# A hybrid decoder layer: both key halves of a stick-breaking head in one accumulator, one stick tile per row, softmax sums added once per head

## The chip, the cores and the metric

The kernel runs on one core of one Trainium2 chip. The metric is the device time of one execution in microseconds (us), and lower is better. The core has four engines that compute: TensorE (PE in the profile, with its weight loads as PEld), VectorE (DVE), ScalarE (ACT) and GpSimd (POOL). SyncE (SP) issues the transfers.

## The reference, cut to what matters

One layer with 2048 tokens and width 1024. A normalised input is projected for two groups of eight heads that work side by side: causal softmax attention over low-rank latents (MLA, group 0), and stick-breaking attention (group 1). Both outputs are normalised, joined, projected back to the residual, and a gated feed-forward layer follows. The stick-breaking group is

```python
z = jnp.einsum("bhqd,bhkd->bhqk", qb.astype(jnp.float32), kf) * scale
log_beta = jax.nn.log_sigmoid(z)
log_one_minus = jnp.where(strict, jax.nn.log_sigmoid(-z), 0.0)
suffix = lax.cumsum(log_one_minus, axis=3, reverse=True) - log_one_minus
a = jnp.where(strict, jnp.exp(log_beta + suffix), 0.0)
return jnp.einsum("bhqk,bhkd->bhqd", a, vf)
```

so that the weight of a key is its own sigmoid times the product of the sigmoids of the negated scores of all later keys: a running product from the last key to the first. Its output is a plain sum over keys, where softmax needs the row's maximum and sum.

## The kernel before, in words

**Stages.** The 2048 tokens are four blocks (b = 0 to 3) of 512, each of four rows (r) of 128. `ORDER` (L87) lists the stages: projections P0 to P3, attention A0 to A3, feed-forward F0, F1, and F for blocks 2 and 3 as a pair by a seven-product scheme. Every operand is split into a high and a low part, and three products replace one.

**Order of the work.** Nothing is issued while these stages are written down. Each call on `plan` is recorded as a task (`record`, L205) with the earlier tasks that it needs, a rank that comes from its stage, and a planned cost (`price`, L243). `order` (L288) then plays a list schedule over five engines: of the tasks that are ready in the plan, an engine takes the one with the lowest key. A transfer counts as landed `DMA_DONE` (L68, used at L412) after its planned time on the wire. `issue` (L458) emits the instructions in that order, and each engine works through its own list strictly in that order. So planned costs set which dense product stands between which attention steps, and an engine whose next instruction is not ready waits, whatever else is ready. The plan also hands out buffers: eight PSUM banks, of which one (`O_B`, L51) is for the attention output `ot`, two for scores, two for transposes, and the others for dense products (`acc`).

**Attention.** `attention` (L781) goes through heads and both groups. Keys come in halves of `SW` = 1024, the later half (c0 = 1024) first; only blocks 2 and 3 have two halves. Each half is a `Unit` (L696): it loads keys and values, and `step` (L774) runs its four rows. A row has one or two pieces of up to 512 keys (`pieces`, L602).

`mla_row` (L632), for each piece: scores into PSUM, `reduce_max` on VectorE; then with two pieces the maximum of both, a scaling `nm`, an exponential on ScalarE per piece with its row sum, and an add of the two sums into `sm`.

`sb_row` (L658), last piece first: scores, two sigmoids on ScalarE, then the running product (`tensor_tensor_scan`) on VectorE into a tile `tb` of 513 columns, whose last column holds what the later piece left: 1, a copy of the later piece's first column, or a copy of the `carry` of the later half. GpSimd then multiplies it into `p`. Two `tb` tiles exist (`NT_BUFS`, L60).

`mix` (L607) takes two rows at a time: it transposes `p` on TensorE into `pt`, splits it (`ph` on ScalarE, `pl` on VectorE), and adds `v` times it into `ot`. After the fourth row `finish` (L727) copies `ot` to `os` (ScalarE), transposes it with four transposes (TensorE, `po`), adds its two parts (ScalarE copy, VectorE add), and keeps the result (`o1`) if it was the first half, or joins both halves and stores it. For stick-breaking the join is one more VectorE add.

`fop_places` (L1016) lists the places for feed-forward operands of the last stage, which lie in attention's buffers once it is over; among them were two `nb` and two `tb` tiles.

Of the kernel before, what the change touches and what calls it, by code (L numbers as in the profile page):

```python
# [66 lines left out]
DMA_RATE = 300.0  # L67
DMA_DONE = 910.0  # L68
NORM_LATE = 1
# [113 lines left out]
class Plan:  # L183
# [21 lines left out]
    def record(self, engine, method, args, kwargs):  # L205
# [8 lines left out]
        for k, v in views:  # L214
            write = k in (first, "accum_out")
            base, region = v.base, v.region or v.base.whole
            if base not in t.bases:
                t.bases.append(base)
            for old, oreg, owrite in base.seen:
                if k == first and engine == "tensor" == old.engine and kwargs.get("start"):  # L220
                    t.needs.add(old.index)
                if (write or owrite) and old is not t and all(a < d and c < b for (a, b), (c, d) in zip(region, oreg)):
                    t.needs.add(old.index)
            if write:
                base.seen = [s for s in base.seen if s[0] is t or not all(a <= c and d <= b for (a, b), (c, d) in
                                                                           zip(region, s[1]))]
            base.seen.append((t, region, write))
        for b in t.bases:
            b.uses += 1
# [13 lines left out]
    def price(self, t):  # L243
# [3 lines left out]
        if t.engine == "tensor":  # L247
# [3 lines left out]
            if t.method == "transpose":  # L251
                cost = 109 if exact else 60
            else:
                cost = 160 if exact else max(58, 10 + 0.4246 * n)
        elif t.engine == "scalar":
# [220 lines left out]
def layer(ctx, tc, x, positions, inv_freq, norm_mix, w_in, q_latent_norm, w_uq,  # L476
# [73 lines left out]
    with ExitStack() as s:  # L550
# [55 lines left out]

        def mix(ot, r0, rows, v, c0):  # L607

            at = [{k0 // P + i: p[:, i * P:(i + 1) * P] for p, k0, n in row for i in range(n // P)} for row in rows]
            js = sorted(at[1])  # L610
            for ja in js[::2]:
# [11 lines left out]
                for half in (ph, pl):  # L623
                    x = 0
                    for j, rs in pair:
                        w = len(rs) * P
                        o0 = (r0 + rs[0]) * P
                        plan.tensor.matmul(ot[:, o0:o0 + w], lhsT=v[:, j - c0 // P, :], rhs=half[:, x:x + w],
                                           start=j == js[0] and half is ph, stop=j == js[-1] and half is pl)
                        x += w  # L630

        def mla_row(r, b, c0, k, q, mx, sm):  # L632
            rs_ = slice(r * P, (r + 1) * P)
            lhs = [(q[0][:, rs_], k, c0), (q[1][:, rs_], k, c0), (q[2][:, rs_], kr, 0)]
            m2 = wk.tile([P, 2], F32, tag="m2", name="m2", bufs=3)
            nm = wk.tile([P, 1], F32, tag="nm", name="nm", bufs=3)
            s2 = wk.tile([P, 2], F32, tag="s2", name="s2", bufs=3)
            parts = pieces(b, r, c0)
# [10 lines left out]
            for i, (k0, n, last) in enumerate(parts):  # L649
                p = pp.tile([P, 512], F32, tag="p", name="p")  # L650
                to = s2[:, i:i + 1] if len(parts) == 2 else sm[:, r:r + 1]
                plan.scalar.activation(p[:, :n], pss[i][:, :n], AF.Exp, bias=nm, scale=SC_M, accum_out=to)
                res.append((p, k0, n))
            if len(parts) == 2:
                plan.vector.tensor_tensor(out=sm[:, r:r + 1], in0=s2[:, 0:1], in1=s2[:, 1:2], op=ALU.add)
            return res

        def sb_row(r, b, c0, k, q, carry, carry_out):  # L658
            rs_ = slice(r * P, (r + 1) * P)
            lhs = [(q[0][:, rs_], k, c0), (q[1][:, rs_], k, c0)]  # L660
            after = None if carry is None else carry[:, r:r + 1]
            res = []
            for k0, n, last in reversed(pieces(b, r, c0)):
                p = pp.tile([P, 512], F32, tag="p", name="p")
                ps = sp.tile([P, 512], F32, tag="s", name="ps_s")
                scores(ps, k0, n, False, lhs)
                tb = wk.tile([P, 513], F32, tag="tb", name="tb", bufs=NT_BUFS)
                plan.scalar.activation(p[:, :n], ps[:, :n], AF.Sigmoid, scale=SC_S)
                plan.scalar.activation(ps[:, :n], ps[:, :n], AF.Sigmoid, scale=-SC_S)
                if after is None:  # L670
                    plan.vector.memset(tb[:, n:n + 1], 1.0)
                else:
                    plan.vector.tensor_copy(tb[:, n:n + 1], after)
                rev, other = ps[:, :n][:, ::-1], p[:, :n][:, ::-1]
                if last:
                    d = n - P
                    plan.gpsimd.tensor_tensor(out=p[:, d:n], in0=p[:, d:n], in1=below, op=ALU.mult)
                    plan.vector.tensor_tensor_scan(tb[:, d:n][:, ::-1], rev[:, :P], beyond[:, ::-1], tb[:, n:n + 1],
                                                 op0=ALU.mult, op1=ALU.max)
                    if d:  # L680
                        plan.vector.tensor_tensor_scan(tb[:, :d][:, ::-1], rev[:, P:], other[:, P:], tb[:, d:d + 1],
                                                     op0=ALU.mult, op1=ALU.bypass)
                else:
                    plan.vector.tensor_tensor_scan(tb[:, :n][:, ::-1], rev, other, tb[:, n:n + 1],
                                                 op0=ALU.mult, op1=ALU.bypass)
                plan.gpsimd.tensor_tensor(out=p[:, :n], in0=p[:, :n], in1=tb[:, 1:n + 1], op=ALU.mult)
                after = tb[:, 0:1]
                res.append((p, k0, n))
            if carry_out is not None:
                plan.vector.tensor_copy(carry_out[:, r:r + 1], after)  # L690
            return res
# [4 lines left out]
        class Unit:  # L696
# [11 lines left out]
            def rows(self, c0, k, v):  # L708
                self.c0, self.v, self.p = c0, v, []
                if self.g == 0:  # L710
                    self.mx = st.tile([P, BT], F32, tag="mx", name="mx")
                    self.sm = st.tile([P, BT], F32, tag="sm", name="sm")
                    return [lambda r=r: mla_row(r, self.b, c0, k, self.q, self.mx, self.sm) for r in range(BT)]
# [4 lines left out]
            def add(self, r, res):  # L718
                self.p.append(res)
                if r % 2:  # L720
                    if r == 1:
                        self.ot = op.tile([P, TB], F32, tag="ot", name="ot")
                    mix(self.ot, r - 1, self.p[-2:], self.v, self.c0)
                if r == BT - 1:
                    self.finish()

            def finish(self):  # L727
# [9 lines left out]
                plan.scalar.activation(po, pt[:, :, :VD], AF.Copy)  # L737
                plan.vector.tensor_tensor(out=po, in0=pt[:, :, VD:], in1=po, op=ALU.add)
                if self.c0:
                    self.o1 = po  # L740
                    return
                o = None if self.g else wk.tile([P, BT, VD], F32, tag="o", name="o")
                if self.g:
                    o = po
                    if self.prev:
                        plan.vector.tensor_tensor(out=o, in0=po, in1=self.prev.o1, op=ALU.add)
                else:
# [4 lines left out]
                    else:  # L752
                        o1, m1, s1 = self.prev.o1, self.prev.mx, self.prev.sm
                        top = st.tile([P, BT], F32, tag="top", name="top")
                        f = st.tile([P, 2, BT], F32, tag="f", name="f")
                        plan.vector.tensor_tensor(out=top, in0=self.mx, in1=m1, op=ALU.max)
                        plan.vector.tensor_tensor(out=f[:, 0], in0=self.mx, in1=top, op=ALU.subtract)
                        plan.vector.tensor_tensor(out=f[:, 1], in0=m1, in1=top, op=ALU.subtract)
                        plan.scalar.activation(f, f, AF.Exp, scale=SC_M)
                        plan.vector.tensor_tensor(out=den, in0=f[:, 0], in1=self.sm, op=ALU.mult)  # L760
# [251 lines left out]
        def place(pool, tag, n):  # L1012
            bufs = {"rt": RT_BUFS, "ph": PH_BUFS, "pl": PH_BUFS, "nb": NT_BUFS, "tb": NT_BUFS}.get(tag)
# [515 lines left out]
```

## Time and profile before

| what | us |
|---|---|
| three runs | 3042.35, 3046.29 (median), 3048.05 |
| the profiled execution, its own time | 3046.05 |
| its span, first to last instruction | 3044.3 |
| TensorE busy in it | 2966.1 |
| VectorE, ScalarE, GpSimd busy | 2382.7, 1786.1, 574.8 |

Busy TensorE means that at least one matmul was in flight. All instructions have the line of the function that emits the plan, so they are told apart by the names of their tiles: `os<-ot` is the copy of the attention output, `po<-ident,os` its transposes, and so on. Attention runs from about 146 us to 1945 us of the span, with projections and feed-forward work of other blocks between its steps; behind it only feed-forward work and output projections are left.

### The profile page before, as it was taken

To read this page: it belongs to the slowest core of one execution; us is meant where nothing else is said; L and a number is where in the kernel's file an instruction comes from. 1 tells how busy PE (TensorE), PEld (TensorE's weight loads), DVE (VectorE), ACT (ScalarE), POOL (GpSimd) and SP (SyncE) were. 2 spreads that over 40 slices of the span, in tenths; PEclk is the share of its full clock that TensorE was granted. 3 is DMA by queue.
4 is the path that set the end of the run, shared out by engine and by line. 5 is a ranking of instruction groups with operands and counts; after the bars stand their busy time and mean duration, and the time that the engine had idled before them with its cause. 6 is when DMAs were issued, how large, how long until landed. Compare 5 with 4: busy or idle time off the path is not lost.

```text
span 3044.3 us, 47607 instructions
## 1 busy us (share of the span) xinstructions
PE 2966.1 (97%) x16372; PEld 2544.5 (84%) x16372; DVE 2382.7 (78%) x4927; ACT 1786.1 (59%) x3858; POOL 574.8 (19%) x619
## 2 busy tenths in 40 slices
PE   8899999999999999999999999999999999999998
PEld 7889888888888888888888888888888788888887
DVE  6567878888989889798978889655657877777777
ACT  5557777777777767777767677544534333233323
POOL 0002221222313314140504123000003100100111
PEclk9999999999999999999999999999999999999999
DMA  6987876677574434434333535355633312111212
GB/s 201 267 259 229 254 224 191 189 226 230 155 206 124 128 108 135 140 117 146 112 105 119 154 118 175 112 176 166 187 110 119 112 55 63 49 48 50 63 49 83
DMA packets 403432, 437.78 MB, mean 144 GB/s; under 512 B 76875, under 2 KB 296054, under 8 KB 403190
## 3 DMA queue, kind: packets, MB, share of 16 engines
q1 hardware_dynamic: 403190, 434.74, 47.3%
q8 instruction: 129, 2.11, 0.3%
q14 instruction: 113, 0.93, 0.1%
HBM read 350.78 MB, written 83.89 MB: 143 GB/s over the span
## 4 chain that ended last, share of the span: by engine, by line
PE 85%; DVE 5%; DMA 5%; ACT 3%; issue 1%; SPq 0%; POOL 0%; ACTq 0%; POOLq 0%; DVEq 0%
PE ps_gu L472 15%; PE ps_d L472 15%; PE ps_m L472 14%; PE ps_s L472 10%; PE ot L472 8%; PE pt L472 7%; PE ps_o L472 5%; PE ps_q L472 5%; PE ps_v L472 2%; PE ps_lat L472 2%; DVE tb L472 1%; PE po L472 1%; PE ps_t L472 1%; DVE acc L472 1%; DMA raw<-in_w_in 1%
## 5 line engine op out<-in xcount | busy, mean ns | idle before, releaser
L472 ACT ACTIVATE whi<-raw 128x512 fp32r<-128x512 f32 (+1 forms) x726 | 448.3, 626 | 581.9 <-PE ps_d L472 208.9
L472 DVE TENSOR_TENSOR wlo<-raw,whi 128x512 fp32r<-128x512 f32 (+1 forms) x726 | 527.2, 734 | 184.9 <-ACT whi L472 177.5
L472 ACT ACTIVATE ph<-pt 128x512 fp32r<-128x512 f32 (+1 forms) x576 | 315.8, 577 | 137.0 <-PE pt L472 123.0
L472 POOL TENSOR_TENSOR p<-p,tb 128x512 f32<-128x512 f32 (+3 forms) x320 | 326.6, 1021 | 351.4 <-DVE tb L472 337.0
L472 PE MATMUL ps_s<-k,q 128*128 128x512 f32 (+3 forms) x1280 | 380.8, 375 | 11.6 <-DMA k<-d_mk 7.3
L472 DVE TENSOR_TENSOR pl<-pt,ph 128x512 fp32r<-128x512 f32 (+1 forms) x576 | 369.9, 650 | 26.3 <-ACT ph L472 23.5
L472 PE MATMUL pt<-ident,p 128*128 128x128 f32 x2176 | 365.5, 275 | 6.2 <-POOL p L472 4.3
L472 PE MATMUL ps_m<-fop,whi 128*128 128x512 f32 (+1 forms) x1254 | 358.8, 375 | 0.0
L472 DVE TENSOR_TENSOR_SCAN tb<-ps_s,tb,p 128x512 f32<-128x512 f32 (+3 forms) x288 | 315.4, 1096 | 6.6 <-ACT ps_s L472 3.1
L472 DVE TENSOR_TENSOR acc<-acc,ps_d 128x512 f32<-128x512 f32 x352 | 235.2, 681 | 78.5 <-PE ps_d L472 74.8
L472 PE MATMUL ps_gu<-tl,whi 128*128 128x512 f32 x704 | 282.8, 402 | 0.0
L472 PEld LDWEIGHTS pt<-ident,p 128*128 128x128 f32 x2176 | 259.7, 141 | 26.6 <-POOL p L472 5.5
L472 PE MATMUL ps_gu<-th,whi 128*128 128x512 f32 x704 | 281.9, 401 | 0.0
L472 PE MATMUL ps_gu<-th,wlo 128*128 128x512 f32 x704 | 281.6, 400 | 0.0
L472 PE MATMUL ps_d<-whi,hh 128*128 128x512 f32 x704 | 278.5, 396 | 0.6 <-ACT hh L472 0.6
L472 PE MATMUL ps_d<-wlo,hh 128*128 128x512 f32 x704 | 277.6, 394 | 0.0
L472 PE MATMUL ps_d<-whi,hl 128*128 128x512 f32 x704 | 272.8, 394 | 0.0
L472 PEld LDWEIGHTS ps_m<-fop,whi 128*128 128x128 f32 x1254 | 227.6, 189 | 45.6
L472 PEld LDWEIGHTS ps_s<-k,q 128*128 128x128 f32 x1280 | 225.1, 190 | 45.3 <-DMA k<-d_mk 7.7
L472 PE MATMUL ot<-pl,v 128*128 128x256 f32 (+1 forms) x1152 | 245.9, 293 | 3.2 <-DVE pl L472 2.3
L472 PE MATMUL ot<-ph,v 128*128 128x256 f32 (+1 forms) x1152 | 232.9, 283 | 12.9 <-ACT ph L472 12.6
L472 PEld LDWEIGHTS ot<-pl,v 128*128 128x128 f32 x1152 | 201.7, 192 | 38.6 <-DVE pl L472 6.5
(222 smaller groups left out, 6178.0 us busy)
## 6 DMA issues: line engine op xcount, KB each, us to landing
raw<-in_w_gate SPq DMA_DIRECT2D x66, 512.0 KB, 4.6
raw<-in_w_up SPq DMA_DIRECT2D x66, 512.0 KB, 3.8
raw<-in_w_down SPq DMA_DIRECT2D x66, 512.0 KB, 3.7
raw<-in_w_o SPq DMA_DIRECT2D x64, 512.0 KB, 4.0
raw<-in_w_in SPq DMA_DIRECT2D x48, 512.0 KB, 5.5
q<-d_mq SPq DMA_DIRECT2D x64, 256.0 KB, 5.3
q<-d_sbq SPq DMA_DIRECT2D x64, 256.0 KB, 5.3
k<-d_mk SPq DMA_DIRECT2D x32, 512.0 KB, 5.4
```

Of the source, the lines that this page charges most:

```text
L472: getattr(getattr(nc, t.engine), t.method)(*args, **kwargs)
```

## The change

The plan's constants: a transfer is planned to land 1.09 us later, a matmul of 128 columns at 108 ns in place of 64, a transpose of a split operand at 86 ns in place of 60. In `record`, every matmul into an accumulator needs the one that began it, and the one that ends it needs all others; steps between are no longer ordered among rows.

For a stick-breaking head of blocks 2 and 3, the second half goes on in the first half's `ot`: `finish` runs once. `sb_row` has one `tb` of 1025 columns for a row; the second piece starts from the column that the first one wrote. `mla_row` takes the maximum of both pieces and the scaling in one instruction, keeps the sums of both pieces apart in a `sm` twice as wide, and `finish` adds them once for the four rows. The merge of two MLA halves works on negated, scaled maxima (min for max, and the exponential's scale -1; not shown). The `nb` places go, and each `tb` holds two operands.

```diff
-DMA_DONE = 910.0
+DMA_DONE = 2000.0
...
             for old, oreg, owrite in base.seen:
-                if k == first and engine == "tensor" == old.engine and kwargs.get("start"):
+                if k == first and engine == "tensor" == old.engine and (kwargs.get("start") or kwargs.get("stop")):
                     t.needs.add(old.index)
...
+        if engine == "tensor" and method == "matmul":
+            if kwargs["start"]:
+                t.out.base.begun = t.index
+            else:
+                t.needs.add(t.out.base.begun)
...
             if t.method == "transpose":
-                cost = 109 if exact else 60
+                cost = 109 if exact else 86
             else:
-                cost = 160 if exact else max(58, 10 + 0.4246 * n)
+                cost = 216 if exact else max(108, 10 + 0.4268 * n)
...
-        def mix(ot, r0, rows, v, c0):
+        def mix(ot, r0, rows, v, c0, first=True, last=True):
...
                         plan.tensor.matmul(ot[:, o0:o0 + w], lhsT=v[:, j - c0 // P, :], rhs=half[:, x:x + w],
-                                           start=j == js[0] and half is ph, stop=j == js[-1] and half is pl)
+                                           start=first and r0 == 0 and j == js[0] and half is ph,
+                                           stop=last and r0 > 0 and j == js[-1] and half is pl)
...
         def mla_row(r, b, c0, k, q, mx, sm):
...
-                plan.vector.reduce_max(out=m2[:, i:i + 1] if len(parts) == 2 else m, in_=ps[:, :n], axis=AX.X)
-                pss.append(ps)
-            if len(parts) == 2:
-                plan.vector.tensor_tensor(out=m, in0=m2[:, 0:1], in1=m2[:, 1:2], op=ALU.max)
-            plan.vector.tensor_scalar(nm, m, -SC_M, None, op0=ALU.mult)
-            for i, (k0, n, last) in enumerate(parts):
+                plan.vector.reduce_max(out=m2[:, i:i + 1], in_=ps[:, :n], axis=AX.X)
+                pss.append((ps, k0, n))
+            if len(pss) == 2:
+                plan.vector.tensor_scalar(m, m2[:, 0:1], m2[:, 1:2], -SC_M, op0=ALU.max, op1=ALU.mult)
+            else:
+                plan.vector.tensor_scalar(m, m2[:, 0:1], -SC_M, None, op0=ALU.mult)
+            for i, (ps, k0, n) in enumerate(pss):
                 p = pp.tile([P, 512], F32, tag="p", name="p")
-                to = s2[:, i:i + 1] if len(parts) == 2 else sm[:, r:r + 1]
-                plan.scalar.activation(p[:, :n], pss[i][:, :n], AF.Exp, bias=nm, scale=SC_M, accum_out=to)
+                plan.scalar.activation(p[:, :n], ps[:, :n], AF.Exp, bias=m, scale=SC_M, accum_out=sm[:, i, r:r + 1])
                 res.append((p, k0, n))
-            if len(parts) == 2:
-                plan.vector.tensor_tensor(out=sm[:, r:r + 1], in0=s2[:, 0:1], in1=s2[:, 1:2], op=ALU.add)
...
         def sb_row(r, b, c0, k, q, carry, carry_out):
...
+            tb = wk.tile([P, SW + 1], F32, tag="tb", name="tb", bufs=NT_BUFS)
...
-                tb = wk.tile([P, 513], F32, tag="tb", name="tb", bufs=NT_BUFS)
...
-                if after is None:
-                    plan.vector.memset(tb[:, n:n + 1], 1.0)
-                else:
-                    plan.vector.tensor_copy(tb[:, n:n + 1], after)
+                if a + n == w:
+                    if carry is None:
+                        plan.vector.memset(tb[:, w:w + 1], 1.0)
+                    else:
+                        plan.vector.tensor_copy(tb[:, w:w + 1], carry[:, r:r + 1])
...
-                    plan.vector.tensor_tensor_scan(tb[:, :n][:, ::-1], rev, other, tb[:, n:n + 1],
+                    plan.vector.tensor_tensor_scan(tb[:, a:a + n][:, ::-1], rev, other, tb[:, a + n:a + n + 1],
                                                  op0=ALU.mult, op1=ALU.bypass)
-                plan.gpsimd.tensor_tensor(out=p[:, :n], in0=p[:, :n], in1=tb[:, 1:n + 1], op=ALU.mult)
-                after = tb[:, 0:1]
+                plan.gpsimd.tensor_tensor(out=p[:, :n], in0=p[:, :n], in1=tb[:, a + 1:a + n + 1], op=ALU.mult)
...
             def add(self, r, res):
...
+                    more = self.g == 1 and self.prev is not None
                     if r == 1:
-                        self.ot = op.tile([P, TB], F32, tag="ot", name="ot")
-                    mix(self.ot, r - 1, self.p[-2:], self.v, self.c0)
-                if r == BT - 1:
+                        self.ot = self.prev.ot if more else op.tile([P, TB], F32, tag="ot", name="ot")
+                    mix(self.ot, r - 1, self.p[-2:], self.v, self.c0, not more, not self.g or not self.c0)
+                if r == BT - 1 and not (self.g and self.c0):
                     self.finish()
...
+                if not self.g:
+                    if len(self.p[0]) == 2:
+                        plan.vector.tensor_tensor(out=self.sm[:, 0], in0=self.sm[:, 0], in1=self.sm[:, 1], op=ALU.add)
+                    self.sm = self.sm[:, 0]
...
                 if self.g:
                     o = po
-                    if self.prev:
-                        plan.vector.tensor_tensor(out=o, in0=po, in1=self.prev.o1, op=ALU.add)
...
         def fop_places():
-                   [[(wk, t)] for t in ("ph", "pl")] * PH_BUFS + [[(wk, t)] for t in ("nb", "tb")] * NT_BUFS)
+                   [[(wk, t)] for t in ("ph", "pl")] * PH_BUFS)
+            for _ in range(NT_BUFS):
+                two = wk.tile([P, 2, TB], F32R, tag="tb", name="fop", bufs=NT_BUFS)
+                one += [two[:, 0], two[:, 1]]
```

## Rows read from the trace of the kernel before

**Rows 1.** The page, busy time, share and instructions of each engine, whole span.
```profile
PE 2966.1 (97%) x16372; PEld 2544.5 (84%) x16372; DVE 2382.7 (78%) x4927; ACT 1786.1 (59%) x3858; POOL 574.8 (19%) x619
```

**Rows 2.** Stretches: from:to, us, busy PE, PEld, DVE, ACT, POOL; PEclk; DMA share; GB/s.
```profile
0.00:200.00 200.00, 177.31 (x955) 156.51 (x956) 124.02 (x329) 113.64 (x276) 9.57 (x20) 0.97 0.80 237
200.00:600.00 400.00, 380.88 (x2499) 342.36 (x2498) 322.64 (x828) 294.19 (x732) 88.69 (x122) 0.99 0.75 222
600.00:1000.00 400.00, 385.61 (x2438) 336.57 (x2436) 351.46 (x807) 299.66 (x688) 101.56 (x117) 0.99 0.62 189
1000.00:1700.00 700.00, 699.93 (x4162) 608.26 (x4161) 605.04 (x1293) 502.30 (x1065) 205.35 (x212) 1.00 0.40 120
1700.00:1950.00 250.00, 244.43 (x1415) 209.39 (x1414) 209.01 (x455) 177.53 (x384) 52.99 (x55) 0.99 0.47 144
```

**Rows 3.** Waits of PE over the span: us in total, times, longest.
```profile
PE ot L472 <- ACT ph L472: 12.6, 11, 2.3
...
PE ps_s L472 <- DMA k<-d_mk: 7.3, 1, 7.3
PE pt L472 <- POOL p L472: 4.3, 4, 2.4
PE po L472 <- ACT os L472: 3.6, 6, 1.1
...
PE ps_s L472 <- DVE tb L472: 2.6, 5, 0.9
...
PE ps_t L472 <- DVE acc L472: 2.4, 3, 1.8
PE ot L472 <- DVE pl L472: 2.3, 6, 0.9
```

**Rows 4.** Timeline of PE behind a stick-breaking first half of block 3 (start us, us).
```profile
1479.61 0.60 PE L472 MATMUL po<-ident,os 128*128 128x128 f32 x4
1479.97 0.48 PE L472 MATMUL ps_s<-k,q 128*128 128x512 f32 x1
...
1481.88 0.40 PE L472 MATMUL ot<-ph,v 128*128 128x256 f32 x2
```

**Rows 5.** Timeline of PE at another end of a unit (start us, us).
```profile
780.83 0.60 PE L472 MATMUL po<-ident,os 128*128 128x128 f32 x4
781.27 0.49 PE L472 MATMUL pt<-ident,p 128*128 128x128 f32 x3
```

**Rows 6.** Groups of ScalarE: names, shapes, count | busy us, mean ns | idle before.
```profile
L472 ACT ACTIVATE os<-ot 128x512 f32<-128x512 f32 x96 | 57.4, 598 | 28.6 <-PE ot L472 25.4 <-DVE rot L472 2.9
L472 ACT ACTIVATE po<-po 128x256 f32<-128x256 f32 x96 | 36.9, 385 | 29.3 <-PE po L472 29.2
```

**Rows 7.** Groups of VectorE, the same columns.
```profile
L472 DVE TENSOR_TENSOR po<-po 128x256 f32<-128x256 f32 x112 | 46.7, 417 | 5.5 <-ACT po L472 4.3
...
L472 DVE TENSOR_TENSOR_SCAN tb<-ps_s,tb,p 128x384 f32<-128x384 f32 x32 | 32.2, 1006 | 0.2
...
L472 DVE TENSOR_SCALAR nm<-mx 128x1 f32<-128x1 f32 x192 | 27.8, 146 | 1.4
...
L472 DVE TENSOR_TENSOR sm<-s 128x1 f32<-128x1 f32 x128 | 20.3, 159 | 81.8 <-ACT p L472 81.5
L472 DVE TENSOR_TENSOR mx<-m 128x1 f32<-128x1 f32 x128 | 20.0, 156 | 1.4
...
L472 DVE COPY tb<-tb 128x1 f32<-128x1 f32 x128 | 18.5, 144 | 1.1
```

**Rows 8.** The chain in order of time: start us, us, what.
```profile
84.94 4.68 DMA d_mk<-ol
89.68 5.50 DMA k<-d_mk
```

**Rows 9.** The page, GpSimd's costliest group, the same columns.
```profile
L472 POOL TENSOR_TENSOR p<-p,tb 128x512 f32<-128x512 f32 (+3 forms) x320 | 326.6, 1021 | 351.4 <-DVE tb L472 337.0
```

**Rows 10.** Timeline of ScalarE at the first half of rows 4 (start us, us).
```profile
1478.51 0.59 ACT L472 ACTIVATE os<-ot 128x512 f32<-128x512 f32 x1
```

More of the change, by code (lines that the diff above doesn't have):

```diff
@@ L635, in mla_row @@
             m2 = wk.tile([P, 2], F32, tag="m2", name="m2", bufs=3)
-            nm = wk.tile([P, 1], F32, tag="nm", name="nm", bufs=3)
-            s2 = wk.tile([P, 2], F32, tag="s2", name="s2", bufs=3)
-            parts = pieces(b, r, c0)
             pss, res = [], []
             m = mx[:, r:r + 1]
-            for i, (k0, n, last) in enumerate(parts):
+            for i, (k0, n, last) in enumerate(pieces(b, r, c0)):
                 ps = sp.tile([P, 512], F32, tag="s", name="ps_s")
                 scores(ps, k0, n, last, lhs)
-                plan.vector.reduce_max(out=m2[:, i:i + 1] if len(parts) == 2 else m, in_=ps[:, :n], axis=AX.X)
-                pss.append(ps)
-            if len(parts) == 2:
-                plan.vector.tensor_tensor(out=m, in0=m2[:, 0:1], in1=m2[:, 1:2], op=ALU.max)
-            plan.vector.tensor_scalar(nm, m, -SC_M, None, op0=ALU.mult)
-            for i, (k0, n, last) in enumerate(parts):
+                plan.vector.reduce_max(out=m2[:, i:i + 1], in_=ps[:, :n], axis=AX.X)
[5 more added lines that the diff above has]
+            for i, (ps, k0, n) in enumerate(pss):
                 p = pp.tile([P, 512], F32, tag="p", name="p")
-                to = s2[:, i:i + 1] if len(parts) == 2 else sm[:, r:r + 1]
-                plan.scalar.activation(p[:, :n], pss[i][:, :n], AF.Exp, bias=nm, scale=SC_M, accum_out=to)
+                plan.scalar.activation(p[:, :n], ps[:, :n], AF.Exp, bias=m, scale=SC_M, accum_out=sm[:, i, r:r + 1])
                 res.append((p, k0, n))
-            if len(parts) == 2:
-                plan.vector.tensor_tensor(out=sm[:, r:r + 1], in0=s2[:, 0:1], in1=s2[:, 1:2], op=ALU.add)
             return res
@@ L660, in sb_row @@
             lhs = [(q[0][:, rs_], k, c0), (q[1][:, rs_], k, c0)]
-            after = None if carry is None else carry[:, r:r + 1]
+            parts = pieces(b, r, c0)
+            w = parts[-1][0] + parts[-1][1] - c0
+            tb = wk.tile([P, SW + 1], F32, tag="tb", name="tb", bufs=NT_BUFS)
             res = []
-            for k0, n, last in reversed(pieces(b, r, c0)):
+            for k0, n, last in reversed(parts):
+                a = k0 - c0
                 p = pp.tile([P, 512], F32, tag="p", name="p")
@@ L677, in sb_row @@
                     plan.gpsimd.tensor_tensor(out=p[:, d:n], in0=p[:, d:n], in1=below, op=ALU.mult)
-                    plan.vector.tensor_tensor_scan(tb[:, d:n][:, ::-1], rev[:, :P], beyond[:, ::-1], tb[:, n:n + 1],
-                                                 op0=ALU.mult, op1=ALU.max)
+                    plan.vector.tensor_tensor_scan(tb[:, a + d:a + n][:, ::-1], rev[:, :P], beyond[:, ::-1],
+                                                 tb[:, a + n:a + n + 1], op0=ALU.mult, op1=ALU.max)
                     if d:
-                        plan.vector.tensor_tensor_scan(tb[:, :d][:, ::-1], rev[:, P:], other[:, P:], tb[:, d:d + 1],
-                                                     op0=ALU.mult, op1=ALU.bypass)
+                        plan.vector.tensor_tensor_scan(tb[:, a:a + d][:, ::-1], rev[:, P:], other[:, P:],
+                                                     tb[:, a + d:a + d + 1], op0=ALU.mult, op1=ALU.bypass)
                 else:
-                    plan.vector.tensor_tensor_scan(tb[:, :n][:, ::-1], rev, other, tb[:, n:n + 1],
+                    plan.vector.tensor_tensor_scan(tb[:, a:a + n][:, ::-1], rev, other, tb[:, a + n:a + n + 1],
                                                  op0=ALU.mult, op1=ALU.bypass)
-                plan.gpsimd.tensor_tensor(out=p[:, :n], in0=p[:, :n], in1=tb[:, 1:n + 1], op=ALU.mult)
-                after = tb[:, 0:1]
+                plan.gpsimd.tensor_tensor(out=p[:, :n], in0=p[:, :n], in1=tb[:, a + 1:a + n + 1], op=ALU.mult)
                 res.append((p, k0, n))
             if carry_out is not None:
-                plan.vector.tensor_copy(carry_out[:, r:r + 1], after)
+                plan.vector.tensor_copy(carry_out[:, r:r + 1], tb[:, 0:1])
             return res
@@ L711, in rows @@
                     self.mx = st.tile([P, BT], F32, tag="mx", name="mx")
-                    self.sm = st.tile([P, BT], F32, tag="sm", name="sm")
+                    self.sm = st.tile([P, 2, BT], F32, tag="sm", name="sm")
                     return [lambda r=r: mla_row(r, self.b, c0, k, self.q, self.mx, self.sm) for r in range(BT)]
@@ L755, in finish @@
                         f = st.tile([P, 2, BT], F32, tag="f", name="f")
-                        plan.vector.tensor_tensor(out=top, in0=self.mx, in1=m1, op=ALU.max)
+                        plan.vector.tensor_tensor(out=top, in0=self.mx, in1=m1, op=ALU.min)
                         plan.vector.tensor_tensor(out=f[:, 0], in0=self.mx, in1=top, op=ALU.subtract)
                         plan.vector.tensor_tensor(out=f[:, 1], in0=m1, in1=top, op=ALU.subtract)
-                        plan.scalar.activation(f, f, AF.Exp, scale=SC_M)
+                        plan.scalar.activation(f, f, AF.Exp, scale=-1.0)
                         plan.vector.tensor_tensor(out=den, in0=f[:, 0], in1=self.sm, op=ALU.mult)
@@ L1012, in place @@
         def place(pool, tag, n):
-            bufs = {"rt": RT_BUFS, "ph": PH_BUFS, "pl": PH_BUFS, "nb": NT_BUFS, "tb": NT_BUFS}.get(tag)
+            bufs = {"rt": RT_BUFS, "ph": PH_BUFS, "pl": PH_BUFS}.get(tag)
             return pool.tile([P, n], F32R, tag=tag, name="fop", bufs=bufs)
```

## The prediction

> **What bounds the kernel now.** First the page's busy times: TensorE has a matmul in flight for 2966.1 of 3044.3 us, 97%, and VectorE is busy for 78% [rows 1]. So TensorE's own work is the bound, and 3044.3 - 2966.1 = 78.2 us are idle. Second, the stretches, which say where those lie [rows 2]: 22.7 us idle in the first 200 us (200.00 - 177.31), 19.1 in 200 to 600, 14.4 in 600 to 1000, 0.1 in 1000 to 1700, 5.6 in 1700 to 1950. Attention lies in the last four of these stretches and the end of the first. In its middle TensorE never lacks work, since the plan puts dense products between the steps; there VectorE is busy for 605 of 700 us and nobody pays for its delays. In 200 to 1000 us the feed of attention is late 33.5 us in all. Third, who was late [rows 3]: `ph` from ScalarE (12.6 us), `p` from GpSimd (4.3), the copy `os` (3.6), `tb` (2.6) and `pl` (2.3) from VectorE, together 25.4 us; and one wait of 7.3 us for keys from memory.
>
> The consequence: TensorE's list is in order and full, so work taken from it shortens the run wherever it lies; work taken from another engine only pays through those 25.4 us.
>
> **TensorE loses four transposes per joined head.** Eight heads in blocks 2 and 3 make 16 first halves whose `finish` goes: 64 transposes. Behind such a half they hold TensorE from 1479.61 to 1479.97, 0.36 us [rows 4]; elsewhere from 780.83 to 781.27, 0.44 us [rows 5]. 16 times that is 5.8 or 7.0 us; I take the middle, **6.4 us**. All other matmuls stay, and a gap left by a transpose is closed by the next instruction in the list, so this term is the surest.
>
> **ScalarE** loses 16 copies `os` of 598 ns and 16 copies `po` of 385 ns [rows 6]: 15.7 us, which it has to spare (59% busy).
>
> **VectorE** loses, by [rows 7]: 128 adds of the two sums (159 ns, 20.4 us); 128 maxima (156 ns, 20.0 us), since one instruction does maximum and scaling and I cost it as the scaling before (146 ns); 128 copies of a first column between two `tb` tiles (144 ns, 18.4 us); and of the 112 adds `po<-po` (96 units and 16 joins) the 16 of the first halves and the 16 joins (417 ns, 13.3 us). It gains one add of four columns per MLA unit with two pieces, 4 per head, 32 in all (5.1 us at 159 ns). Net 67.0 us. More important is a wait: VectorE sat idle for 81.5 us before those sum adds, because each stood in its list right behind an exponential that was not done [rows 7]. With 32 in place of 128, three quarters of it, 61 us, should go. So some 128 us of VectorE's list open up. The plan prices a one-column operation at about 67 ns (`price`) where it takes 144 to 159, so some 350 fewer of them also keep the real order of events nearer to the planned one.
>
> What is it worth? The waits on VectorE's own results (2.6 and 2.3) I let go whole, and a sixth of the waits for `os`, as 16 of 96 copies go: 5.5 us. Of the 16.9 us on `ph` and `p`, made by engines that only follow VectorE at a distance, I let go the share that the 128 us have in the 1750 us of 200 to 1950: 7%, 1.2 us. Together 6.7, rounded to **7 us**; the bounds are 0 (other waits take their place) and 25.4.
>
> **The plan's constants.** Each transfer is now planned to land 1.09 us later. The one long wait for memory is a chain of two, a store of 4.68 us and the load behind it of 5.50 us [rows 8]; between them the plan moves this step by 2.2 us. I take **2.2 us** of the 7.3, with bounds 0 (the weights of the projections that would fill the hole are planned later as well) and 7.3. The prices of short matmuls change the order, and I can't price that: zero, with the first 200 us as likely to lose as to win.
>
> The Trainium skill (SBUF — State Buffer, The DMA setup-cost knee) gives a transfer a fixed cost of about 2 us plus its bytes over 436 GB/s. By that the load would be an estimated 2.6 us for 256 KB, the new constant would be right, all 7.3 us would go and the sum would be 20.7 in place of 15.6. The trace does not agree: 5.50 us.
>
> **Costed at nothing.** Wider `sm` and `tb` tiles change no instruction's size; `nb` gives up the space that `tb` takes. Two `tb` tiles of two pieces each let the first scan of a row start without a free tile per piece; that is in the `tb` waits above. Minimum for maximum is one for one. In `mix`, the loss of order between rows removes waits within TensorE's own list, where none show. No transfer is added or moved by hand. **An added wait**: the next unit's `ot` comes free only after the second half; it was one bank before as well.
>
> **Sum.** 6.4 + 7 + 2.2 = 15.6 us off 3046.05, the profiled execution's own time, 0.24 us below the median of the three runs: 3030.4, so **3030 us**. A change of less than 0.2%, some 6.1 us, can't be told from none here.
>
> **Rivals.**
> A. The forecast, chance 0.48, 3022 to 3037.
> B. Only the transposes count: a new order deals the waits out anew, with the same sum. 3046.05 - 6.4 = 3039.7, just on the bound between faster and same. For it: the idle of 200 to 1000 is many short waits for many things. Chance 0.18.
> C. VectorE's blocked time was behind most of the late feed: all 25.4 and 7.3 go. 3046.05 - 6.4 - 32.7 = 3007. Against it: half of the 25.4 waits for ScalarE, which is little changed. Chance 0.12.
> D. Slower. Both pieces of a row now lie in one `tb`. If the scan of the second piece is held until GpSimd has read the first one's part, VectorE's list stands still for up to 1.02 us [rows 9] on each of 128 second pieces, 131 us, and everything behind (`pl`, `wlo`, accumulations) with it. If that makes 1000 to 1950 as tight as 200 to 1000 (33.5 of 800, 4.2%), TensorE idles 39.8 us there in place of 5.7: 3046.05 - 6.4 + 34.1 = 3074. Against it: the scanned and the read columns don't overlap, and before, where GpSimd masks one part of `p` while a scan reads another, those scans show 0.2 us of idle time in 32 [rows 7]. It decides only when the blocked time is more than the 128 us opened plus what VectorE has idle (262 us in 200 to 1950 by rows 2). Chance 0.10.
> E. The bank that came free in mid-head is gone: from the end of `os` (1478.51 + 0.59) [rows 10] to the next `ot` at 1481.88 [rows 4], 2.8 us, 16 times. If each time a dense tile misses it and TensorE waits as it did for accumulations (2.4 us in 3 waits, 0.8 each [rows 3]), that is 12.8 us: 3046.05 - 6.4 + 12.8 = 3052, slightly slower. Against it: 0.1 us idle in 1000 to 1700, where most of these halves lie. Chance 0.06. The Trainium skill (PSUM — Partial Sum Buffer, Summary: rules for kernel authors) speaks for this one: "Evacuate promptly". The trace shows no wait that a longer-held bank explains.
> F. No change: the new order loses at the start, where 22.7 us are idle already, what the transposes give. 3046. Chance 0.06.
>
> **How the numbers follow.** The time is A's. Faster: A, C and half of B, 0.69. Same: half of B, F and a third of E, 0.17. Slower: D and the rest of E, 0.14. The range leaves out D, E and the deepest third of C (0.10 + 0.06 + 0.04 = 0.20): 3010 to 3046.
>
> **What would show it.** Right: 320 `po` transposes in place of 384; TensorE's busy time down by some 6 us; the idle time before the sum adds down to some 20 us; idle in 200 to 1000 below 33.5 us; the load of keys in the first 100 us waited for less than 7.3 us. Wrong: `tb` scans with idle time on GpSimd's `p` (D); idle in 1000 to 1700 with waits for an accumulator (E); equal idle sums spread over other names (B); TensorE's mean clock or matmul durations changed, which no step above foresees.

## The result, and the profile after

The changed kernel takes 3015.8 us (median of five runs, 3013.0 to 3020.55) against 3047.15 (median of five): a ratio of 0.9901 with a 95% interval of 0.9887 to 0.9916, some 30 us off. The forecast was 3030 in a range of 3010 to 3046. The profiled execution is the slowest of the five, 3020.55 us, with a span of 3018.7, so its trace shows 25.6 us of the gain (3044.3 - 3018.7).

The page's busy times, as in [rows 1]:

```profile
PE 2955.4 (98%) x16308; PEld 2530.6 (84%) x16308; DVE 2329.4 (77%) x4543; ACT 1771.6 (59%) x3826; POOL 573.4 (19%) x619
```

TensorE is busy for 10.7 us less and idle for 63.3 us in place of 78.2, 14.9 less. The stretches, with the columns of [rows 2]:

```profile
0.00:200.00 200.00, 184.15 (x982) 161.69 (x983) 125.05 (x330) 113.16 (x277) 10.04 (x20) 0.98 0.81 242
200.00:600.00 400.00, 380.96 (x2530) 343.29 (x2530) 324.22 (x797) 300.36 (x745) 101.26 (x136) 0.98 0.72 218
600.00:1000.00 400.00, 386.51 (x2499) 334.33 (x2497) 354.86 (x764) 321.24 (x740) 113.81 (x131) 1.00 0.62 192
1000.00:1700.00 700.00, 698.19 (x4232) 607.41 (x4231) 599.25 (x1162) 514.81 (x1106) 197.46 (x209) 1.00 0.41 123
1700.00:1950.00 250.00, 249.49 (x1258) 210.04 (x1258) 169.45 (x299) 131.18 (x259) 35.00 (x32) 1.00 0.46 143
```

Idle time per stretch is now 15.9, 19.0, 13.5, 1.8 and 0.5 us, against 22.7, 19.1, 14.4, 0.1 and 5.6. So little was won in 200 to 1000 us (32.5 against 33.5), 6.8 us in the first 200, and 5.1 in the last stretch, where less attention is left: the last copy `os` begins at 1774.3 us, as the next fence shows in its last columns, and before the change it began at 1941.4. The stretches are cut by time, not by work: the changed kernel gets through 92 more matmuls, of mixed sizes, in 200 to 1000 us (5029 against 4937) with nearly the same idle time. The view of the tile `ot`, its copy before and after (min/median/max in ns, first and last start in us):

```profile
L472 ACT ACTIVATE os<-ot x96: 579/597/676, 236.2 to 1941.4; 128x512 f32<-128x512 f32 x96
...
L478 ACT ACTIVATE os<-ot x80: 578/598/651, 227.9 to 1774.3; 128x512 f32<-128x512 f32 x80
```

The waits of TensorE, as in [rows 3]:

```profile
PE po L478 <- ACT os L478: 8.4, 8, 2.0
...
PE ot L478 <- ACT ph L478: 5.1, 5, 2.7
PE pt L478 <- POOL p L478: 3.8, 5, 1.2
...
PE ps_s L478 <- DMA k<-d_mk: 2.8, 1, 2.8
PE ot L478 <- DVE pl L478: 2.7, 7, 0.7
...
PE ps_s L478 <- DVE tb L478: 1.9, 4, 0.6
```

The groups of VectorE, as in [rows 7], and below them the transposes on TensorE, before and after:

```profile
L478 DVE TENSOR_SCALAR mx<-m 128x1 f32<-128x1 f32 x192 | 36.0, 189 | 2.1
...
L478 DVE TENSOR_TENSOR po<-po 128x256 f32<-128x256 f32 x80 | 33.2, 414 | 21.2 <-ACT po L478 21.1
L478 DVE TENSOR_TENSOR_SCAN tb<-ps_s,tb,p 128x384 f32<-128x384 f32 x32 | 32.3, 1010 | 0.3
...
L478 DVE TENSOR_TENSOR sm<-sm 128x4 f32<-128x4 f32 x32 | 5.5, 172 | 13.2 <-ACT p L478 12.9
```

```profile
L472 PE MATMUL po<-ident,os 128*128 128x128 f32 x384 | 58.0, 273 | 3.6 <-ACT os L472 3.6
...
L478 PE MATMUL po<-ident,os 128*128 128x128 f32 x320 | 48.7, 274 | 8.5 <-ACT os L478 8.4
```

Of the 128 adds of sums that waited 81.8 us, 32 are left that wait 13.2. The 128 copies between two `tb` are gone, `po<-po` counts 80 in place of 112, the `po` transposes 320 in place of 384. The scaling that also takes the maximum is dearer than the old one: 64 rows of one piece at 146 ns [rows 7] leave 26.7 us for the other 128, 208 ns each (an estimate from 192 x 189 ns).

### The profile page after: what moved, and what is told of

Its sections match the earlier page's. It is cut to its first block, busy times and chain, and to the rows that moved or that the text cites. A ratio compares the mean times of both kernels' runs of the same rounds, so it can differ in the third digit from the quotient of the medians.

```text
span 3018.7 us, 46993 instructions
## 1 busy us (share of the span) xinstructions
PE 2955.4 (98%) x16308; PEld 2530.6 (84%) x16308; DVE 2329.4 (77%) x4543; ACT 1771.6 (59%) x3826; POOL 573.4 (19%) x619
## 4 chain that ended last, share of the span: by engine, by line
PE 84%; DVE 8%; DMA 3%; ACT 3%; issue 2%; SPq 0%; POOL 0%; POOLq 0%; ACTq 0%; DVEq 0%
PE ps_d L478 15%; PE ps_gu L478 14%; PE ps_m L478 14%; PE ps_s L478 9%; PE ot L478 7%; PE pt L478 6%; PE ps_o L478 5%; PE ps_q L478 5%; DVE tb L478 2%; PE ps_v L478 2%; DVE pl L478 1%; PE ps_lat L478 1%; PE po L478 1%; PE ps_t L478 1%; DVE wlo L478 1%
## 5 line engine op out<-in xcount | busy, mean ns | idle before, releaser
L478 DVE TENSOR_TENSOR wlo<-raw,whi 128x512 fp32r<-128x512 f32 (+1 forms) x726 | 512.2, 714 | 220.5 <-ACT whi L478 211.1
L478 PE MATMUL pt<-ident,p 128*128 128x128 f32 x2176 | 359.4, 274 | 6.4 <-POOL p L478 3.8
L478 DVE TENSOR_REDUCE m<-ps_s 128x1 f32<-128x512 f32 (+2 forms) x320 | 188.5, 605 | 67.2 <-PE ps_s L478 66.5
```

The source lines that it names most:

```text
L478: getattr(getattr(nc, t.engine), t.method)(*args, **kwargs)
```

## The experiments

The edits of the change fall into three groups: work removed, a later planned landing of transfers, and new prices of TensorE's instructions. "Work" takes in all that isn't a constant, the new rule on the order of accumulating matmuls and the places of operands too; no run separates these. The prices take in the one of an exact fp32 matmul (160 to 216) and the slope per column. Twelve kernels take the groups apart. In the table, "waits" is the sum of the rows in the views of ScalarE's and VectorE's waits that end with a transfer; the ratio is to the kernel before on the same chip.

| run | work | landing | prices | median us | ratio, 95% interval | waits us |
|---|---|---|---|---|---|---|
| before | as before | 910 | old | 3044 to 3047 | 1 | 104 |
| the change | removed | 2000 | new | 3015.8 | 0.9901 (0.9887 to 0.9916) | 97 |
| e1 | removed | 910 | old | 3033.47 | 0.9970 (0.9958 to 0.9982) | 128 |
| e2 | as before | 2000 | new | 3027.58 | 0.9946 (0.9934 to 0.9959) | 85 |
| e3 | removed | 910 | new | 3040.65 | 0.9993 (0.9984 to 1.0002) | 138 |
| e4 | removed | 2000 | old | 2995.68 | 0.9842 (0.9829 to 0.9856) | 90 |
| n4 | removed | 1500 | old | 3016.65 | 0.9903 (0.9887 to 0.9920) | 92 |
| n3 | removed | 3000 | old | 2988.60 | 0.9817 (0.9802 to 0.9831) | 50 |
| w4 | removed | 4000 | old | 3001.46 | 0.9861 (0.9847 to 0.9876) | 41 |
| w1 | as before | 2000 | old | 3033.91 | 0.9967 (0.9956 to 0.9979) | 81 |
| n1 | removed | 2000 | old, slope 0.4268 | 2999.21 | 0.9849 (0.9835 to 0.9864) | 91 |
| n2 | removed | 2000 | old, floor 108 | 3005.56 | 0.9870 (0.9855 to 0.9885) | 75 |
| w2 | all but the shared accumulator | 2000 | old | 3008.36 | 0.9885 (0.9870 to 0.9900) | 78 |
| w3 | all but the sums per head | 2000 | old | 3004.20 | 0.9871 (0.9856 to 0.9886) | 83 |

**Work or plan?** The theories were W (the removed work makes the gain) and P (beyond the transposes it is the plan's constants); with later runs came L (a later landing takes waits for transfers away), S (a wrong price costs what it is wrong by) and R (any changed constant deals the order of the instructions out anew, and times scatter by that). e1 is the changed kernel with

```diff
-DMA_DONE = 2000.0
+DMA_DONE = 910.0
...
-                cost = 109 if exact else 86
+                cost = 109 if exact else 60
...
-                cost = 216 if exact else max(108, 10 + 0.4268 * n)
+                cost = 160 if exact else max(58, 10 + 0.4246 * n)
```

> The changed kernel with the plan's old constants (landing 910, short matmuls 64 ns, split transposes 60 ns). Theory W (the removed work makes the gain): 3016 to 3024 us, attention over near 1775 us, idle before 200 us still near 22 us or a little less. Theory P (beyond the transposes' 6.4 us the gain is the constants'): 3034 to 3041 us.

It took 3033.47 us: W's 3016 to 3024 is missed by 9 us, and P's band, which begins at 3034, by 0.5. 0.30% are 9 us (5 to 13), for the work alone. The last copy `os` begins at 1788 us all the same, so attention is over earlier with the removed work, and that by itself pays little:

```profile
L478 ACT ACTIVATE os<-ot x80: 580/598/679, 238.2 to 1788.2; 128x512 f32<-128x512 f32 x80
```

e2 is the kernel before with the three lines reversed:

> The kernel before with the plan's new constants alone. Theory W: 3042 to 3050 us, attention over near 1942 us as before. Theory P: 3020 to 3032 us, and the idle time of TensorE in the first 200 us falls from 22.7 to near 16 us.

3027.58 us, inside P's band, and TensorE's idle time in the first 200 us falls to 17.4: constants alone are worth 0.54%, some 16 us (12 to 20). The third and the fourth put one group of constants back in the changed kernel, e3 the landing (910), e4 the prices (60, 160, 58 and 0.4246):

> The changed kernel with transfers planned to land as before (910). Theory W: 3011 to 3020 us. Theory P, if the landing time is its part: 3022 to 3032 us, with the wait of 7 us for the first keys back.

> The changed kernel with the old prices of TensorE's instructions (new landing time). Theory W: 3011 to 3020 us. Theory P, if the prices are its part: 3022 to 3032 us.

e3 lies beyond P's band too: without the landing time next to nothing of the gain is left. The wait for the first keys is back, as expected:

```profile
PE ps_s L478 <- DMA k<-d_mk: 7.0, 1, 7.0
```

e4 is neither's: it is 20 us faster than the change. With the work removed, then, the later landing pays (37.8 us from e1 to e4; 24.9 from e3 to the change, 28 by the ratios), and the new prices cost (7.2 us from e1 to e3; 20.1 from e4 to the change, 18 by the ratios). With the work as before, two runs of the table show otherwise: the landing alone (w1) pays 10 us, and the new prices on top of it (w1 to e2, 3033.91 to 3027.58) pay 6 more. So the landing time pays in all three pairs, by 10 to 38 us, and the prices have no settled sign. The kernel before with the new prices and the old landing was not run.

**Where the landing time acts.** The stretch of 200 to 1000 us of e1, with the columns of [rows 2]:

```profile
200.00:1000.00 800.00, 764.69 (x4986) 677.41 (x4985) 668.73 (x1538) 606.51 (x1455) 200.86 (x257) 0.99 0.68 206
```

and the same stretch of e4:

```profile
200.00:1000.00 800.00, 779.40 (x5116) 695.93 (x5115) 686.45 (x1571) 620.41 (x1483) 211.68 (x260) 1.00 0.69 210
```

35.3 us idle fall to 20.6, and 130 more matmuls are in the stretch. Over the whole span TensorE's idle time falls from 77.9 to 55.4 us, and its busy time from 2953.8 to 2940.1 with the same matmuls. ScalarE's waits for transfers in the kernel before, four of eleven rows (us in total, times, longest):

```profile
ACT whi L472 <- DMA raw<-in_w_in: 27.0, 14, 7.9
...
ACT whi L472 <- DMA raw<-in_w_gate: 14.5, 7, 3.3
...
ACT junk L472 <- DMA xt<-in_x: 12.1, 5, 3.7
ACT oh L472 <- DMA d_sbk<-oh: 10.6, 6, 4.4
```

The two uppermost kinds of them in e1:

```profile
ACT whi L478 <- DMA raw<-in_w_in: 28.7, 13, 7.3
...
ACT whi L478 <- DMA raw<-in_w_gate: 13.9, 8, 2.6
```

in e4:

```profile
ACT whi L478 <- DMA raw<-in_w_in: 13.4, 8, 5.0
...
ACT whi L478 <- DMA raw<-in_w_gate: 8.7, 6, 2.2
```

and in n3, a kernel that comes below:

```profile
ACT whi L478 <- DMA raw<-in_w_in: 9.8, 7, 5.3
...
ACT whi L478 <- DMA raw<-in_w_gate: 6.9, 4, 3.3
```

ScalarE squares a row of input (`junk`), splits a weight tile (`whi`) and refills a buffer that a store has read (`oh`, `vt`) when the transfer has landed. Planned to land too early, such an instruction stands in ScalarE's list ahead of others and waits there for memory. One place in the kernel before, on ScalarE's timeline (start us, us, and in brackets the idle time before):

```profile
342.92 0.63 ACT L472 ACTIVATE junk<-xt 128x512 bf16<-128x512 f32 x1 [3.70 <-DMA xt<-in_x]
...
345.34 0.96 ACT L472 ACTIVATE ph<-pt 128x512 fp32r<-128x512 f32 x2
```

and on TensorE's:

```profile
343.45 0.40 PE L472 MATMUL ps_s<-k,q 128*128 128x512 f32 x1
345.97 0.50 PE L472 MATMUL ot<-ph,v 128*128 128x256 f32 x2 [2.12 <-ACT ph L472]
```

The row of `xt` is 3.70 us late, the `ph` some places behind it in the list starts at 345.34 in its turn, and TensorE stands still for 2.12 us under the name of `ph`; this is one of the 12.6 us of [rows 3]. Counted over the trace, 7 of the 18 waits of TensorE for ScalarE of over 0.3 us (9.2 of 19.9 us) come within 4.5 us behind such a wait of ScalarE, a distance chosen for the count. In e1 it is 7 of 21 (10.0 of 19.8 us), in e4 5 of 16 (5.0 of 13.1), in n3 none of 11, but in the changed kernel 6 of 14 (9.9 of 14.8). The wait for `ph` in e1:

```profile
PE ot L478 <- ACT ph L478: 12.5, 13, 2.6
```

and in e4:

```profile
PE ot L478 <- ACT ph L478: 4.6, 5, 1.7
```

One place on this route is shown, then, and the count gives it some 5 of the 22 us of idle time between e1 and e4; the rest is spread over many names. Between the kernel before and the change the route carries nothing (9.2 and 9.9 us). To see whether the size of the step counts, the old prices were kept and the landing time of e4 set to 3000 (n3), 1500 (n4) and 4000 (w4):

```diff
-DMA_DONE = 2000.0
+DMA_DONE = 3000.0
```

> The changed kernel with the old prices and a landing time of 3000 in place of 2000. Theory L (later planned landing takes away waits of ScalarE and VectorE for transfers, some 38 us from 910 to 2000): these waits fall below the 89.5 us at 2000, and the time is 2985 to 3000 us. Theory R: 2995 to 3020 us while the waits fall or stay.

> The changed kernel with the old prices and a landing time of 1500. Theory L: between the 3033 us at 910 and the 2996 us at 2000, so 3008 to 3020 us, with waits of ScalarE and VectorE for transfers between 128 and 89.5 us. Theory R: anywhere in 2995 to 3033 us, with no tie to the waits.

> The changed kernel with the old prices and a landing time of 4000. Theory L: the gain flattens once the planned landing is near the measured ones: 2980 to 2992 us, waits of ScalarE and VectorE for transfers at or below the 50 us of 3000. If the plan now holds work back for transfers that have long landed: 2995 to 3015 us.

910, 1500, 2000 and 3000 give 3033, 3017, 2996 and 2989 us, in the order that theory L foresees, and n3 and its waits (50 us) are inside L's bands. n4's time is in L's band, but its waits are hardly above those of 2000 (92 against 90), so the waits for transfers are not the whole of it. Nor do they order the kernels of the table: w1 waits 81 us and takes 3033.91, the change waits 97 and takes 3015.8. At 4000 L's band is missed: the waits fall once more (41) and the time rises by 13 us, as the other expectation has it. One row that grows, by 2.8 us of the 13, is TensorE's wait for VectorE's `tb`. In n3:

```profile
PE ps_s L478 <- DVE tb L478: 4.3, 8, 0.9
```

and in w4:

```profile
PE ps_s L478 <- DVE tb L478: 7.1, 13, 1.1
```

That the plan holds work back for transfers that have landed, and that this is why, is not shown; a new deal of the order is the other candidate.

**Prices or a new deal?** A changed constant deals the order out anew, so a run that changes one by next to nothing shows what one new deal alone does. n1 takes e4 with a slope of 0.4268 in place of 0.4246, n2 takes e4 with a floor of 108 in place of 58:

```diff
-                cost = 160 if exact else max(58, 10 + 0.4246 * n)
+                cost = 160 if exact else max(58, 10 + 0.4268 * n)
```

> The changed kernel with the old prices of TensorE's instructions, but the slope per column 0.4268 in place of 0.4246: a matmul of 512 columns is planned 1.1 ns longer, and the order is dealt anew. Theory R (the 20 us between old and new prices are the scatter of newly dealt orders): anywhere in 2995 to 3020 us, by 8 us or more away from 2996. Theory S (a price that is wrong costs what it is wrong by): 2993 to 2999 us.

> The changed kernel with the old prices, but short matmuls planned at 108 ns in place of 64. Theory S, if this price is the one that costs: 3010 to 3020 us. Theory R: anywhere in 2995 to 3020 us, with no tie to the step made.

n1 is at 2999.21 us, 3.5 over e4: outside S's band by 0.2 us and far less than R's 8. n2 is at 3005.56, 9.9 over e4: less than S foresaw, and inside R's wide band. n1's order is a new one: by the names of the tiles, half of TensorE's matmuls stand elsewhere in its list than in e4. So one new deal was worth 3.5 us (2 by the ratios), and the executions of both kernels overlap (2996.96 to 3002.15 against 2992.41 to 2997.25). It is one draw. How far other deals scatter is not shown, and prices that cost 20 us in one pair and pay 6 in another speak for more than 3.5. So R is not ruled out for the prices, nor as a part of every other step here. Which of the prices makes up the 20 is not settled either.

**The parts of the work, with the landing at 2000 and old prices.** w1 is the kernel before with `DMA_DONE = 2000.0` alone:

> The kernel before with the landing time of 2000 alone, all else of the change left out. Theory L: its part of the 2996 us of the changed kernel with old prices is the landing time, the rest the removed work, which is worth 11 us as at 910: 3004 to 3012 us. If work and landing time help each other by more than their sum: 3013 to 3030 us.

3033.91 us, over both bands: the landing alone is worth 0.33%, 10 us, and so is the work alone (e1, 9 us), but both together are worth 1.58%, 48 us (e4). With the old prices they help each other. In 200 to 1000 us w1's TensorE is idle for 32.9 us (800 - 767.08), as before the change, and e1's for 35.3; only both together lower that idle time (e4, 20.6). With the new prices no such help is seen: the change idles there for 32.5 us, the work is worth 12 us from e2 to the change (14 by the ratios), and e1's 9 and e2's 16 nearly make up the 30 of the change. The stretch of w1:

```profile
200.00:1000.00 800.00, 767.08 (x4957) 676.72 (x4956) 681.72 (x1646) 599.72 (x1432) 191.70 (x236) 1.00 0.68 206
```

w2 puts the second accumulator back in e4:

```diff
-                    more = self.g == 1 and self.prev is not None
+                    more = False
...
-                    mix(self.ot, r - 1, self.p[-2:], self.v, self.c0, not more, not self.g or not self.c0)
-                if r == BT - 1 and not (self.g and self.c0):
+                    mix(self.ot, r - 1, self.p[-2:], self.v, self.c0)
+                if r == BT - 1:
...
                     o = po
+                    if self.prev:
+                        plan.vector.tensor_tensor(out=o, in0=po, in1=self.prev.o1, op=ALU.add)
```

> The changed kernel with the old prices, but each half of a stick-breaking head has its own accumulator, copy, transposes and the join again. Theory W (TensorE's work counts one for one): 64 transposes more, 5.8 to 7.0 us over 2995.7, 3000 to 3005 us, with 384 po transposes. If the handover of the accumulator counts besides its work: 3006 to 3015 us.

3008.36 us, 12.7 over e4, with its 384 transposes in TensorE's groups:

```profile
L478 PE MATMUL po<-ident,os 128*128 128x128 f32 x384 | 58.9, 275 | 5.5 <-ACT os L478 4.1 <-DVE thl L478 1.2
```

That is the second expectation's band; but 12.7 less the transposes' 5.8 to 7.0 leaves 6 to 7 us, which the handover, the other copies and adds that come back, and a new deal share; they can't be told apart here. w3 adds the two sums after each row again:

```diff
                 res.append((p, k0, n))
+            if len(pss) == 2:
+                s = sm[:, 0, r:r + 1]
+                plan.vector.tensor_tensor(out=s, in0=s, in1=sm[:, 1, r:r + 1], op=ALU.add)
             return res
...
-                    if len(self.p[0]) == 2:
-                        plan.vector.tensor_tensor(out=self.sm[:, 0], in0=self.sm[:, 0], in1=self.sm[:, 1], op=ALU.add)
```

> The changed kernel with the old prices, but the two sums of a softmax row are added after each row again. Theory W: VectorE's idle time before these adds comes back (60 us or more), and TensorE hardly feels it: 2994 to 3001 us. If VectorE's blocked list is what feeds TensorE late: 3003 to 3015 us.

3004.20 us, 8.5 over e4, in the band of the second expectation. VectorE's waits before these adds in e4:

```profile
DVE sm L478 <- ACT p L478: 14.3, 17, 2.1
```

and in w3:

```profile
DVE sm L478 <- ACT p L478: 49.0, 71, 1.7
```

They rise by 35 us where 60 were expected, and TensorE's idle time in 200 to 1000 us rises from 20.6 to 26.5 (800 - 773.54). The stretch of w3:

```profile
200.00:1000.00 800.00, 773.54 (x5072) 685.30 (x5071) 692.36 (x1607) 622.08 (x1486) 212.59 (x264) 1.00 0.69 208
```

So TensorE idles some 6 us more there, which fits a blocked VectorE, but over the whole span only 2.8 more (58.2 against 55.4), and a new deal alone made 3.5 us in n1. The second expectation's reason is not shown. The single `tb` and the joined maximum and scaling were not undone one by one. Of all runs n3 is the fastest, 2988.6 us: 0.85% below the change (0.9817 over 0.9901).

## Why the prediction was right, and which term was mis-sized

**The direction and the range held; the size was half.** 15.6 us were forecast and some 30 came. 3015.8 lies below the 3022 to 3037 of the forecast's own rival A; the range holds it because it reaches down into rival C. The term that was mis-sized is that of the plan's constants, 2.2 us with bounds of 0 and 7.3. e2 measures it, landing and prices together, at 0.54%, 16 us (12 to 20), beyond its upper bound. The reading behind it was too narrow: it asked which transfers TensorE itself waits for, and one row of 7.3 us answers that [rows 3]. ScalarE and VectorE waited 104 us for transfers in the same trace, and what stood behind in their lists could reach TensorE as a wait for `ph`, as at 345.97 us. But these waits are still 85 us in e2 and 97 in the changed kernel, so how the constants gained their 16 us stays open; a luckier deal of the order may be in it. The load named there changed the way that was foreseen and by more than the 2.2 us: TensorE waited 2.8 us for it in place of 7.3. Its place in the changed kernel's chain (start us, us):

```profile
85.41 6.18 DMA k<-d_mk
```

**The transposes** (6.4 us): 64 fewer, and TensorE's busy time in `po` falls from 58.0 to 48.7 us. w2, which puts them back, costs 12.7 us, with the handover and a new deal in it. Nothing speaks against the term; no run has it alone.

**VectorE's 7 us.** With the transposes it makes 13.4 us of work; e1 measures 9 (5 to 13) with the old constants, and e2 against the change 12 to 14 with the new ones. That sum was about right, then. Net 53.3 us of VectorE's time went (2382.7 - 2329.4) in place of 67.0, in part as the joined instruction takes 208 ns in place of 146. The idle time before the sum adds fell to 13.2 us, somewhat below the 20 foreseen. But the place was wrong: 200 to 1000 us was to gain and kept 32.5 us of its 33.5. The prediction put all of the 33.5 down to the feed of attention, while the rows that it names hold 25.4 us over the whole span. Over the span, `po` waits 8.4 us for the copy `os` where it waited 3.6, while the wait for `ph` falls from 12.6 to 5.1: one late feed in place of another.

**The prices of short matmuls**, "I can't price that: zero". They cost 7 and some 20 us in two pairs of runs and paid 6 in the third. Zero hid a term as large as the others, of either sign.

**The clock.** The prediction lists a changed mean clock of TensorE as a sign of being wrong, and that sign came. The span and the mean granted clock of the kernel before, the change, e1 and e4:

```profile
core 0: 3044.3 us, clock 0.992
...
core 0: 3018.7 us, clock 0.995
...
core 0: 3031.7 us, clock 0.994
...
core 0: 2995.5 us, clock 0.997
```

(1 - 0.992) x 3044.3 is 24.4 us and (1 - 0.995) x 3018.7 is 15.1: an estimate, from these lines alone, of up to 9 of the 25.6 us between the first two traces, and the same working gives 9 of the 36 us between e1 and e4. With a landing of 910 the executions of the kernel before, e1 and e3 have a clock of 0.990 to 0.995, with a landing of 1500 or more 0.994 to 0.998. In the traces of the kernel before and of the change, the clock falls to its lower level (1.2 GHz) during a wait of TensorE or at most 1.1 us behind one, but for the last fall at the very end. One such place in the kernel before, on TensorE's timeline and in two stretches with the columns of [rows 2]:

```profile
259.77 0.50 PE L472 MATMUL ot<-ph,v 128*128 128x256 f32 x2 [1.68 <-ACT ph L472]
...
256.00:260.30 4.30, 2.50 (x19) 2.03 (x18) 3.94 (x9) 3.83 (x12) 0.46 (x1) 1.00 1.05 296
260.30:263.70 3.40, 3.40 (x19) 3.40 (x18) 2.88 (x6) 2.91 (x7) 0.46 (x1) 0.50 1.10 351
```

So waits of TensorE were followed by matmuls at the lower clock in these traces, and the prediction's sum has no term for that. Why some waits are followed by a fall and others not is not shown.

**The rivals.** B (only the transposes count, 3039.7) is out; with the landing time put back, e3 (3040.65) comes near it. C (all late feed goes, 3007) is nearest in size, but not for its reason: the waits for `ph`, `p`, `os`, `tb` and `pl` are still 21.9 us after, with 2.8 for the keys. D is out: the scans of 384 columns show 0.3 us of idle time in 32, and VectorE's waits for GpSimd's `p` under the name of `tb` are 2.1 us in all:

```profile
DVE tb L478 <- POOL p L478: 2.1, 6, 0.6
```

E is out: no wait for an accumulator is among the rows after, 1000 to 1700 idles for 1.8 us, and the run that gives the bank back in mid-head (w2) is slower than e4. "Evacuate promptly", which the Trainium skill says (PSUM — Partial Sum Buffer, Summary: rules for kernel authors), decides nothing here. F is out, as the start gained 6.8 us.

**The rule on transfers.** The Trainium skill (SBUF — State Buffer, The DMA setup-cost knee) would put the landing near 2 us plus the bytes, which is the new constant. The measurement speaks against it as the best value: a load of keys takes 6.18 us in the chain after, and a landing of 3000 beats 2000 by 0.25% (0.9817 against 0.9842), with one deal of the order each.

## What to carry to other kernels

When an order is planned ahead and engines work their lists in order, the plan's constants are an edit of their own, and need a run of their own: here they were worth as much (16 us) as the work that was removed (9 to 14). What one edit is worth depends on the others: the removed work paid 9 us with the old constants, 38 with the later landing alone and 12 to 14 with all new constants, so measure it in the setting in which it will be kept. Add up the waits for memory of every engine, not of the bounding one alone, since a late transfer can arrive at the bounding engine under another engine's name; but don't take their sum for the time (97 us of waits in the change, 81 in the slower w1). Before a change of order is believed, run the same kernel with several constants changed by next to nothing; one such run (3.5 us here) doesn't tell how far new deals scatter. And compare the granted clock of both traces before busy time is put down to work.

## What was not expected of the hardware

A VectorE instruction on one column with two column operands and a constant (maximum, then scaling) took 208 ns, where one with a single column took 146. A group of four transposes of 128 columns holds TensorE for 0.36 us in one place and 0.44 in another [rows 4, 5], so a quarter of it is not a constant.
